# A transformer block on one core: one weight section summed earlier, eight block sums taken out of their product, and the closing row scaling shared out anew

## The chip, the cores and the metric

The kernel runs on one core of one Trainium2 chip. A core has TensorE (PE: matrix products, results in PSUM), VectorE (DVE), ScalarE (ACT), GpSimd (POOL) and SyncE (SP, which here issues most of the DMA transfers). The metric is the device time of one execution in microseconds (us). Three executions of the kernel before took 1255.12, 1257.43 and 1259.67 us, median 1257.43 us.

## The reference

One block of a transformer over 1024 positions of width 1024, in float32: an adaptive normalisation, a mixer with four differential-attention heads and four latent-attention (MLA) heads, a residual with a gate, a second adaptive normalisation, a SwiGLU network, a second gated residual, and a closing normalisation.

```python
mod = c_act @ w_ada[l] + b_ada[l]
sh_a, sc_a, g_a, sh_f, sc_f, g_f = jnp.split(mod[:, None, :], N_MOD, axis=-1)
h = rms_norm(x, g_mix[l]) * (1.0 + sc_a) + sh_a
x = x + g_a * hybrid_mixer(h, w_in[l], ...)
h = rms_norm(x, g_ffn[l]) * (1.0 + sc_f) + sh_f
x = x + g_f * (jax.nn.silu(h @ w_gate) * (h @ w_up)) @ w_down      # D_FF = 2816
return rms_norm(x, g_final)
```

## The kernel before, in words

Each large float32 product is made from three products of rounded halves: an operand is cast by ScalarE to a high part (`dhi`, `whi`), VectorE subtracts to get the low part (`dlo`, `wlo`), both by `split` (L160 to L165, the subtraction is recorded at L158), and TensorE does high by high, high by low and low by high. All tiles that are not small share one pool of 49 slots of 4 KB per partition (`NBUF`, tag "s"); a tile takes a slot when its first instruction is placed and gives it back after its last.

The order of the instructions on an engine is made by a planner. The code emits everything once, and an earlier place in the code is a higher priority; what has its inputs and a slot ready may be placed ahead of what was emitted earlier but is not ready. An instruction passed to `pin` stays behind the instruction that was emitted before it on the same engine. On the chip each engine then works through its list in that order, and waits at an instruction whose input is not there.

Weights come as a `Stream` of items, each a load and a preparation. `pump` emits the next preparation and the loads of the next `ahead` items, `allow` sets how far it may go, `need` goes to a named item at once. The first stream `st` holds what the projections need; `st2` holds w_out and all feed-forward operands.

The stages, in order of time: the input normalisation and the first projections (to 150 us); the latent projections and up-projections as a list `fill`, between which score units of the differential heads are run (150 to 330 us); the other attention units and the first half of the w_out products (to 500 us); w_out and the second normalisation (to 590 us); gate and up products (to 1023 us); down products (to 1243 us); the closing rows.

Section 3 of w_ada (the shift `sh_f`) is 8 loads of 512 KB, each followed by one VectorE multiply-add into `acc` (L339, L341), and after the eighth by 16 small matrix products (L373) and a bias add (L383). It is needed first in the second normalisation. The kernel before keeps it in a stream of its own, `st3`, pumped once in each unit after the first 20, that is while the other attention units run (L1225 to L1227).

The down product uses one level of Strassen's scheme in Winograd's form over the two halves of the 22 rows of blocks: seven products in the order "1256734", each over 11 pairs of blocks c and four row tiles t, three matrix products each (L1484 to L1486). Products alternate between four single PSUM banks (`psb`: 1, 5, 7, 4) and two double ones (`psd`: 2, 6, 3). The operand of product 5 is a sum and a difference of two halves, made by VectorE from two double loads into a tile `stt` (L824 to L827) and then split; products 6, 3 and 4 go on from that tile, and product 7 has two subtractions of its own. `ahead(("dn", i, c), DLEAD)` (L1479) emits preparations up to `DLEAD` items past the one in use and the loads of four items more. Results are taken out of PSUM by closures in `pend`, one after each c (two in product 4): `evac_dn`, `scale` and `base21`. Parts of x1 (the residual) come back from memory by `load_x1`, in product 1 for the row tiles 0 to 3 and in product 7 for the tiles 4 to 7.

In product 4 the last four c are done row tile by row tile, and `last21` (L1455) closes each row: a multiplication by the gate and a subtraction (VectorE, both with an operand in PSUM), a square with its sum (ScalarE), the sum of the two halves' squares (VectorE), two small GpSimd instructions for the reciprocal root, then one half scaled by ScalarE and the other by VectorE, and two DMAs.

Of the kernel before, what the change touches and what calls it, by code (L numbers as in the profile page):

```python
# [10 lines left out]
AF = mybir.ActivationFunctionType  # L11
# [10 lines left out]
LT = 4  # L22
PD = 1
DSP = 2
ALLOW = [(0, 'rope'), (12, ('qup', 2)), (25, None)]
SPILL = 'gpsimd'
DS = 4
ND = 2
# [22 lines left out]
ORD0 = [(1, 1), (0, 1), (0, 2), (1, 2), (0, 2), (0, 0), (0, 0), (0, 0), (1, 0), (1, 0), (1, 0), (1, 0)]  # L51
IT0 = (0, 4, 1, 2, 3, 5, 6, 7)
NLATE = 1
DLEAD = 3


class Stream:
# [40 lines left out]
def emit(ctx, tc, a, out, dbg=None, rec=None):  # L98
# [12 lines left out]
    def slot(shape, dt, name):  # L111
        n = nm(name)
        if rec:
            rec.alloc(n)
        return sp.tile([P] + list(shape), dt, name=n, tag="s", bufs=NBUF)
# [253 lines left out]
    def col_sec(sec, fin):  # L369
        def done(acc):  # L370
            ps = psb()
            for j in range(8):
                pin(mm(ps[:, j:j + 1], lhsT=acc[:, j * 128:(j + 1) * 128], rhs=ones[:, 0:1], start=True, stop=True))  # L373
            fin(ps)

        return ada_items(sec, done)
# [20 lines left out]
    for q in range(3):  # L397
        n = 3 if q < 2 else 2
        witem(st, ("lk", q), win[q * 384:q * 384 + n * 128, 1920:2240].rearrange("(k p) n -> p k n", p=P), [n, 320])
    st.add("rope", load_tabs, lambda: None)  # L400
    for k in range(3):
        witem(st, ("qup", k), a["w_q_up"][k * P:(k + 1) * P, :], [768], nc.gpsimd)
    for k in range(2):
        witem(st, ("kvup", k), a["w_kv_up"][k * P:(k + 1) * P, :], [1024], nc.gpsimd)
    st3 = Stream(2)
    for it in col_sec(3, fin_shf):
        st3.add(*it)


    def x_norm(t):  # L410
# [385 lines left out]
    def dn_item(i, c):  # L796
        key = ("dn", i, c)
        ga = scr["g"][2 * c:2 * c + 2]
        wa = a["w_down"][2 * c * P:(2 * c + 2) * P, :].rearrange("(f p) n -> f p n", p=P)
        g0, g1, w0, w1 = ga[0], ga[1], wa[0], wa[1]  # L800

        def dma():
            r = slot([2, 512], F32, "raw")
            q = None
            if i in "57":
                q = slot([2, 512], F32, "raw")
                if i == "5":
                    ld(out=r, in_=ga[:, :, HI].rearrange("f p t -> p f t"))
                    ld(out=q, in_=w0.rearrange("p (f n) -> p f n", f=2))
                else:  # L810
                    ld(out=r, in_=g0.rearrange("p (f n) -> p f n", f=2))
                    ld(out=q, in_=wa[:, :, HI].rearrange("f p t -> p f t"))
            else:
                x, y = {"1": (g0[:, LO], w0[:, LO]), "2": (g1[:, LO], w1[:, LO]), "6": (g0[:, LO], w1[:, HI]),
                        "3": (g1[:, LO], w1[:, HI]), "4": (g1[:, HI], w1[:, LO])}[i]
                ld(out=r[:, 0, :], in_=x)
                ld(out=r[:, 1, :], in_=y)
            raws[key] = (r, q)

        def prep():  # L820
            r, q = raws.pop(key)
            v = nc.vector
            if i == "5":
                z = stt[c] = slot([2, 512], F32, "stt")  # L824
                v.tensor_tensor(out=z[:, 0, :], in0=r[:, 0, :], in1=r[:, 1, :], op=ALU.add)
                sub(v, z[:, 1, :], q[:, 1, :], q[:, 0, :])
                r = z  # L827
            elif i == "6":
                z = stt[c]
                sub(v, z[:, 0, :], z[:, 0, :], r[:, 0, :])  # L830
                sub(v, z[:, 1, :], r[:, 1, :], z[:, 1, :])
                r = z
            elif i == "7":
                sub(v, r[:, 0, :], r[:, 0, :], r[:, 1, :])
                sub(v, r[:, 1, :], q[:, 1, :], q[:, 0, :])
            elif i == "3":
                sub(v, r[:, 0, :], r[:, 0, :], stt[c][:, 0, :])
            elif i == "4":
                sub(v, r[:, 1, :], stt.pop(c)[:, 1, :], r[:, 1, :])
            hi = slot([2, 512], F32R, "dhi")  # L840
            lo = slot([2, 512], F32R, "dlo")
            split(r, hi, lo)
            W[key] = (hi, lo)

        st2.add(key, dma, prep)
# [62 lines left out]
    ORDER = "1256734"  # L908
    for i in ORDER:
        for c in range(NP):  # L910
            dn_item(i, c)

    def load_t(key, src):
        t = slot([2, 512], F32R, "op")
# [307 lines left out]
    W.clear()  # L1222
    for n in range(done, NS):
        step(n, LA)
        if n > done:  # L1225
            st3.allow()
            st3.pump()  # L1227
        if n - NU in WOL:
            st2.need(("wo", WOL[n - NU]))
        for t in WOD.get(n - NU, []):  # L1230
            wout_d(t)
# [66 lines left out]
    def rest(n, jp):  # L1298
        aop(n, jp, sa[n, jp])
# [154 lines left out]

    def last21(o, t):  # L1455
        t4 = 4 + t
        r = x1[t4]
        vtt(out=o, in0=o, in1=gf[:, LO], op=ALU.mult)
        sub(nc.vector, r[:, LO], r[:, LO], o)
        sq(t4, LO, 0)  # L1460
        ss = ssq[t4]
        vtt(out=ss[:, 0:1], in0=ss[:, 0:1], in1=ss[:, 1:2], op=ALU.add)
        rs = rstd_of(ss[:, 0:1], D)
        nc.scalar.activation(osl[t4][:, HI], r[:, HI], AF.Copy, scale=rs)
        nc.vector.scalar_tensor_tensor(out=osl[t4][:, LO], in0=r[:, LO], scalar=rs, in1=gfin[:, LO], op0=ALU.mult, op1=ALU.mult)
        for half in (HI, LO):
            ld(out=out[t4 * P:(t4 + 1) * P, half], in_=osl[t4][:, half])

    for n, i in enumerate(ORDER):
        if n % 2:  # L1470
            e = [psd() for _ in range(2)]
            o = [e[t // 2][:, t % 2, :] for t in range(4)]
        else:
            o = [psb() for _ in range(4)]
        TL = 7 if i == "4" else NP
        seq = [(c, t) for c in range(TL) for t in range(4)] + [(c, t) for t in range(4) for c in range(TL, NP)]
        for c, t in seq:
            if t == 0:
                ahead(("dn", i, c), DLEAD)  # L1479
                if i in "17" and c in (2, 4, 6, 8):  # L1480
                    load_x1((c - 2) // 2 + (0 if i == "1" else 4))
            hi, lo = W["dn", i, c]
            tt = slice(t * 128, (t + 1) * 128)
            mm(o[t], lhsT=hi[:, 0, tt], rhs=hi[:, 1, :], start=c == 0, stop=False)  # L1484
            mm(o[t], lhsT=hi[:, 0, tt], rhs=lo[:, 1, :], start=False, stop=False)  # L1485
            mm(o[t], lhsT=lo[:, 0, tt], rhs=hi[:, 1, :], start=False, stop=c == NP - 1)  # L1486
            if t == 3:
                del W["dn", i, c]
                for _ in range(2 if i == "4" else 1):
                    if pend:  # L1490
                        pend.pop(0)()
            if i == "4" and c == NP - 1:
                last21(o[t], t)
        if i != "4":
            pend += [lambda i=i, z=z, t=t: evac_dn(i, z, t) for t, z in enumerate(o)]
        if i == "3":
            pend += [lambda t=t: base21(t) for t in range(4)]
    assert not pend


_INS = ["x", "vecs", "ident", "ada_a", "ada_b", "w_ada", "b_ada", "w_in", "rope", "w_q_up", "w_kv_up", "tabs", "lam", "w_out",
# [51 lines left out]
```

## Time and profile before

| | |
|---|---|
| median of three runs | 1257.43 us |
| the profiled execution | 1257.22 us, its span 1255.3 us |
| TensorE busy | 1205.8 us (96%), 5951 products, mean granted clock 0.983 |
| VectorE busy | 829.2 us (66%) |
| ScalarE busy | 494.4 us (39%) |
| GpSimd busy | 439.0 us (35%) |
| chain that ended last | PE 77%, DVE 12%, ACT 4%, no wait shown 4%, DMA 1%, POOL 1% |

All rows are of this one profiled execution, and times in them are microseconds from the start of its span. A busy share over the whole span is a mean over stages with different limits, so the rows below are of single stretches. In a row of instructions the last bracket is the idle time before the first, with what ended it.

### The profile page before, as it was taken

The numbers are of one execution on the slowest core, as the hardware profiler recorded it, in microseconds if no ns is written. First come the engines' busy times: TensorE is split into PE (matmuls) and PEld (weight loads), VectorE is DVE, ScalarE is ACT, GpSimd is POOL, SyncE is SP. The second block draws the span as 40 slices with busy tenths as digits, with TensorE's granted clock in tenths as the row PEclk, the third lists the DMA queues.
The fourth block names the chain that finished last, engine by engine and source line by source line (L and its number), as shares of the span: only waits on it lengthen the run. The fifth ranks groups of instructions, "written<-read, shape, count | busy, mean of one in ns | idle before, by whom it ended". The sixth has DMA issues, their size and how long they took to land.

```text
span 1255.3 us, 16479 instructions
## 1 busy us (share of the span) xinstructions
PE 1205.8 (96%) x5951; PEld 1013.7 (81%) x5951; DVE 829.2 (66%) x1282; ACT 494.4 (39%) x850; POOL 439.0 (35%) x492
## 2 busy tenths in 40 slices
PE   8999999999899999999899999999999999999995
PEld 6888898988679898887688888878888888878774
DVE  6643514477697878768865565665555575699997
ACT  4542225455556665124532223313233244143353
POOL 4420002654243256113455445565444620000112
PEclk9999998999999999999899999999999999999998
DMA  9774842357986434321132233322122369779543
GB/s 369 301 255 167 313 137 74 106 170 227 336 250 166 137 109 144 116 94 59 51 118 96 91 117 125 110 84 84 51 101 84 117 234 393 250 252 327 190 129 135
DMA packets 82972, 209.33 MB, mean 167 GB/s; under 512 B 7805, under 2 KB 18379, under 8 KB 82763
## 3 DMA queue, kind: packets, MB, share of 16 engines
q1 hardware_dynamic: 63611, 168.36, 40.0%
q0 software_dynamic: 6336, 23.07, 4.8%
q10 hardware_dynamic: 12944, 16.84, 3.9%
q8 instruction: 47, 0.77, 0.2%
q14 instruction: 34, 0.28, 0.1%
HBM read 164.21 MB, written 44.04 MB: 166 GB/s over the span
## 4 chain that ended last, share of the span: by engine, by line
PE 77%; DVE 12%; ACT 4%; issue 4%; DMA 1%; POOL 1%; SPq 0%; ACTq 0%; POOLq 0%; DVEq 0%
PE psb L1338 32%; PE psb L439 5%; PE psb L441 5%; PE psb L440 5%; PE psb L481 3%; PE psd L481 3%; PE psd L1485 2%; PE psd L1486 2%; PE psd L1484 2%; PE psb L1030 2%; ACT s L949 2%; PE psb L1485 2%; PE psb L1484 2%; PE psb L1486 2%; DVE dlo L158 1%
## 5 line engine op out<-in xcount | busy, mean ns | idle before, releaser
L1338 PE MATMUL psb<-ah,whi 128*128 128x512 f32 x528 | 143.7, 394 | 2.9 <-ACT uv L1367 2.6
L1338 PE MATMUL psb<-ah,wlo 128*128 128x512 f32 x528 | 142.0, 391 | 0.8 <-DVE wlo L158 0.8
L1338 PE MATMUL psb<-al,whi 128*128 128x512 f32 x528 | 141.7, 390 | 0.4 <-DVE al L158 0.4
L1361 POOL TENSOR_TENSOR cf<-cf,cf 128x512 f32<-128x512 f32 x44 | 66.4, 1510 | 190.5 <-DVE cf L1354 183.9
L1338 PEld LDWEIGHTS psb<-ah,whi 128*128 128x128 f32 x528 | 99.3, 189 | 24.9 <-ACT uv L1367 3.0
L1354 DVE TENSOR_TENSOR cf<-psb,uv 128x512 f32<-128x512 f32 x88 | 60.3, 686 | 89.1 <-PE psb L1338 88.2
L1338 PEld LDWEIGHTS psb<-ah,wlo 128*128 128x128 f32 x528 | 99.6, 189 | 22.1 <-DVE wlo L158 1.2
L1338 PEld LDWEIGHTS psb<-al,whi 128*128 128x128 f32 x528 | 99.0, 188 | 21.4 <-DVE al L158 0.8
L162 ACT CAST whi<-ssum 128x1024 fp32r<-128x1024 f32 x44 | 45.0, 1045 | 166.9 <-POOL ssum L158 166.9
L158 DVE TENSOR_TENSOR wlo<-ssum,whi 128x1024 fp32r<-128x1024 f32 x44 | 62.3, 1416 | 55.5 <-ACT whi L162 55.5
L949 ACT ACTIVATE s<-s,nb 128x640 f32<-128x640 f32 (+7 forms) x96 | 74.4, 777 | 48.9 <-DVE nb L947 48.5
L162 ACT CAST dhi<-raw 128x1024 fp32r<-128x1024 f32 x63 | 64.5, 1051 | 64.5 <-DVE raw L158 29.0
L947 DVE CUSTOM_DVE_ANT_0 s<-psd,tabs 128x640 f32<-128x640 f32 (+7 forms) x80 | 63.3, 803 | 38.2 <-PE psd L973 36.1
L158 DVE TENSOR_TENSOR dlo<-raw,dhi 128x1024 fp32r<-128x1024 f32 x59 | 73.9, 1274 | 15.5 <-ACT dhi L162 15.3
L1485 PE MATMUL psb<-dlo,dhi 128*128 128x512 f32 x176 | 69.0, 392 | 0.1
L439 PE MATMUL psb<-whi,hh 128*128 128x512 f32 (+2 forms) x192 | 68.1, 354 | 1.0 <-ACT latq L638 0.9
L1486 PE MATMUL psb<-dhi,dlo 128*128 128x512 f32 x176 | 68.5, 389 | 0.0
L441 PE MATMUL psb<-whi,hl 128*128 128x512 f32 (+2 forms) x192 | 67.3, 350 | 0.0
L440 PE MATMUL psb<-wlo,hh 128*128 128x512 f32 (+2 forms) x192 | 67.2, 350 | 0.0
L1365 ACT ACTIVATE cf<-cf 128x512 f32<-128x512 f32 x44 | 27.8, 632 | 99.7 <-DVE cf L1354 99.7
L1484 PE MATMUL psb<-dhi 128*128 128x512 f32 x176 | 63.8, 391 | 1.1 <-ACT dhi L162 1.0
L1453 POOL TENSOR_TENSOR x<-x,gfin 128x512 f32<-128x512 f32 x4 | 5.5, 1377 | 164.3 <-ACT o L1417 160.0
(321 smaller groups left out, 3105.9 us busy)
## 6 DMA issues: line engine op xcount, KB each, us to landing
adr<-in_w_ada_dram SPq DMA_DIRECT2D x32, 512.0 KB, 6.4
raw<-scr_g SPq DMA_DIRECT2D x55, 256.0 KB, 3.6
raw<-in_w_down_dram SPq DMA_DIRECT2D x55, 256.0 KB, 4.2
raw<-in_w_gate_dram SPq DMA_DIRECT2D x22, 512.0 KB, 3.3
raw<-in_w_up_dram SPq DMA_DIRECT2D x22, 512.0 KB, 3.3
scr_g<-cf POOLq DMA_DIRECT2D x22, 512.0 KB, 3.2
raw<-scr_g SPq DMA_DIRECT2D x22, 512.0 KB, 5.4
raw<-in_w_down_dram SPq DMA_DIRECT2D x22, 512.0 KB, 6.2
```

Of the source, the lines that this page charges most:

```text
L158: pn(eng.tensor_tensor(out=o, in0=x, in1=y, op=ALU.subtract))
L162: pn(nc.scalar.copy(hi, raw))
L439: mm(o, lhsT=ah, rhs=bh, start=start, stop=False)
L440: mm(o, lhsT=ah, rhs=bl, start=False, stop=False)
L441: mm(o, lhsT=al, rhs=bh, start=False, stop=stop)
L481: pn(mm(o, lhsT=w[z == 2][:, m * 128:(m + 1) * 128], rhs=h[z == 1], start=(k == 0 and z == 0), stop=(k == 7 and z == 2)))
L949: nc.scalar.activation(s, s, AF.Exp, bias=nb[:, m:m + 1], scale=-1.0, accum_out=rs[:, m:m + 1])
L1338: mm(o, lhsT=w[l][:, k, :], rhs=x[2 * (k // 2) + r][:, k % 2, :], start=(l + r == 0 and k == 0), stop=(r == 1 and k == 3))
L1361: nc.gpsimd.tensor_tensor(out=g, in0=g, in1=o, op=ALU.mult)
L1484: mm(o[t], lhsT=hi[:, 0, tt], rhs=hi[:, 1, :], start=c == 0, stop=False)
L1485: mm(o[t], lhsT=hi[:, 0, tt], rhs=lo[:, 1, :], start=False, stop=False)
L1486: mm(o[t], lhsT=lo[:, 0, tt], rhs=hi[:, 1, :], start=False, stop=c == NP - 1)
```

## The change

Three parts. (1) The shift section goes from its own stream into the main one, behind the rope tables and ahead of the up-projection weights; the first `allow` reaches to its end, so its eight items are pumped in the places 4 to 11 of the `fill` list. (2) Product 5's operand is made by separate items "s": for c 0 to 7 they stand at eight places among the items of products 1 and 2 (`EARLY`), for c 8 to 10 just ahead of their use; product 5's item then only splits. The lead in the down product goes from 3 to 6 items, and x1 is loaded in products 2 and 6 instead of 1 and 7. (3) In `last21` the low half is multiplied by the final gain on GpSimd ahead of the scale, the add of the two sums goes to GpSimd, both halves are scaled by ScalarE, and the scaling of a row is emitted after the next row's square; all of it is pinned.

```diff
-ALLOW = [(0, 'rope'), (12, ('qup', 2)), (25, None)]
+ALLOW = [(0, ('ad', 3, 7)), (12, ('qup', 2)), (25, None)]
-DLEAD = 3
+DLEAD = 6
+EARLY = [("1", 3), ("1", 6), ("1", 9), ("2", 1), ("2", 3), ("2", 5), ("2", 7), ("2", 9)]
     st.add("rope", load_tabs, lambda: None)
+    for it in col_sec(3, fin_shf):
+        st.add(*it)
     for k in range(3):
         witem(st, ("qup", k), ...)
...
-    st3 = Stream(2)
-    for it in col_sec(3, fin_shf):
-        st3.add(*it)
...
         def dma():
+            if i == "5":
+                return
             r = slot([2, 512], F32, "raw")
             q = None
-            if i in "57":
+            if i in "s7":
                 q = slot([2, 512], F32, "raw")
...
-            r, q = raws.pop(key)
+            r, q = raws.pop(key, (None, None))
-            if i == "5":
+            if i == "s":
                 z = stt[c] = slot([2, 512], F32, "stt")
                 v.tensor_tensor(out=z[:, 0, :], in0=r[:, 0, :], in1=r[:, 1, :], op=ALU.add)
                 sub(v, z[:, 1, :], q[:, 1, :], q[:, 0, :])
-                r = z
+                return
+            elif i == "5":
+                r = stt[c]
...
     for i in ORDER:
         for c in range(NP):
+            if i == "5" and c >= len(EARLY):
+                dn_item("s", c)
             dn_item(i, c)
+            if (i, c) in EARLY:
+                dn_item("s", EARLY.index((i, c)))
...
         step(n, LA)
-        if n > done:
-            st3.allow()
-            st3.pump()
...
     def last21(o, t):
         t4 = 4 + t
-        r = x1[t4]
-        vtt(out=o, in0=o, in1=gf[:, LO], op=ALU.mult)
-        sub(nc.vector, r[:, LO], r[:, LO], o)
-        sq(t4, LO, 0)
-        ss = ssq[t4]
-        vtt(out=ss[:, 0:1], in0=ss[:, 0:1], in1=ss[:, 1:2], op=ALU.add)
-        rs = rstd_of(ss[:, 0:1], D)
-        nc.scalar.activation(osl[t4][:, HI], r[:, HI], AF.Copy, scale=rs)
-        nc.vector.scalar_tensor_tensor(out=osl[t4][:, LO], in0=r[:, LO], scalar=rs, in1=gfin[:, LO], op0=ALU.mult, op1=ALU.mult)
-        for half in (HI, LO):
-            ld(out=out[t4 * P:(t4 + 1) * P, half], in_=osl[t4][:, half])
+        r, ss, y = x1[t4], ssq[t4], osl[t4]
+        pin(vtt(out=o, in0=o, in1=gf[:, LO], op=ALU.mult))
+        pin(vtt(out=r[:, LO], in0=r[:, LO], in1=o, op=ALU.subtract))
+        pin(nc.scalar.activation(o, r[:, LO], AF.Square, accum_out=ss[:, 0:1]))
+        pin(nc.gpsimd.tensor_tensor(out=y[:, LO], in0=r[:, LO], in1=gfin[:, LO], op=ALU.mult))
+        pin(nc.gpsimd.tensor_tensor(out=ss[:, 0:1], in0=ss[:, 0:1], in1=ss[:, 1:2], op=ALU.add))
+        rs = small(1, "rstd")
+        pin(nc.gpsimd.tensor_scalar(out=rs, in0=ss[:, 0:1], scalar1=1.0 / D, scalar2=EPS, op0=ALU.mult, op1=ALU.add))
+        pin(nc.gpsimd.tensor_tensor(out=rs, in0=rs, in1=mhalf[:, 0:1], op=ALU.pow))
+        for fn in tail:
+            fn()
+
+        def rest():
+            pin(nc.scalar.activation(y[:, HI], r[:, HI], AF.Copy, scale=rs))
+            pin(nc.scalar.activation(y[:, LO], y[:, LO], AF.Copy, scale=rs))
+            for half in (HI, LO):
+                ld(out=out[t4 * P:(t4 + 1) * P, half], in_=y[:, half])
+
+        tail[:] = [rest]
...
-                if i in "17" and c in (2, 4, 6, 8):
-                    load_x1((c - 2) // 2 + (0 if i == "1" else 4))
+                if i in "26" and c in (2, 4, 6, 8):
+                    load_x1((c - 2) // 2 + (0 if i == "2" else 4))
...
-    assert not pend
+    for fn in tail:
+        fn()
```

## Rows read from the trace of the kernel before

**Rows 1.** Windows of the down product: busy us (instructions) by engine, granted clock, DMA share, GB/s.
```profile
1022.90:1082.70 59.80, 59.80 (x265) 49.56 (x264) 33.68 (x33) 18.14 (x20) 3.45 (x4) 1.00 0.95 345
1082.70:1242.90 160.20, 154.68 (x661) 123.84 (x660) 152.08 (x196) 61.84 (x74) 14.54 (x12) 0.99 0.60 206
1173.60:1210.70 37.10, 32.76 (x133) 25.53 (x133) 35.88 (x43) 14.57 (x20) 5.51 (x4) 0.95 0.49 157
1210.70:1242.90 32.20, 31.21 (x133) 24.27 (x131) 30.60 (x41) 12.15 (x18) 9.03 (x8) 1.00 0.28 100
1242.90:1255.30 12.40, 0.04 (x1) 0.00 (x0) 5.62 (x12) 4.84 (x11) 2.95 (x8) 0.66 0.46 170
```
**Rows 2.** Waits of PE in 1170 to 1243 us: us in total, times, longest.
```profile
PE psd L1485 <- DVE dlo L158: 3.4, 3, 1.6
```
**Rows 3.** Timeline of DVE in product 5: start, us, line, tiles.
```profile
1106.96 1.22 DVE L158 TENSOR_TENSOR dlo<-stt,dhi 128x1024 fp32r<-128x1024 f32 x1
1108.10 0.68 DVE L825 TENSOR_TENSOR stt<-raw 128x512 f32<-128x512 f32 x1
1108.70 0.69 DVE L158 TENSOR_TENSOR stt<-raw 128x512 f32<-128x512 f32 x1
```
**Rows 4.** Groups of DVE instructions, first in 1022.9 to 1082.7, then 1082.7 to 1242.9.
```profile
L158 DVE TENSOR_TENSOR dlo<-stt,dhi 128x1024 fp32r<-128x1024 f32 x3 | 3.7, 1225 | 3.5 <-ACT dhi L162 3.5
...
L825 DVE TENSOR_TENSOR stt<-raw 128x512 f32<-128x512 f32 x7 | 4.8, 683 | 0.0
```
**Rows 5.** Window of 1027 to 1077.5 us, and median issue to landing of one load.
```profile
1027.00:1077.50 50.50, 50.50 (x224) 41.85 (x223) 28.70 (x29) 18.14 (x20) 0.00 (x0) 1.00 1.01 372
...
raw<-scr_g SPq DMA_DIRECT2D x55, 256.0 KB, 3.6
```
**Rows 6.** Chain that ended last, 334 to 346 us, then PE's timeline there.
```profile
336.13 7.17 DMA adr<-in_w_ada_dram
...
345.33 0.69 PE L988 MATMUL psb<-E,E 128*128 128x384 f32 x1 [4.00 <-DVE ptl L158]
```
**Rows 7.** Windows in the fill and in the attention units, columns as in Rows 1.
```profile
150.00:175.00 25.00, 25.00 (x125) 22.31 (x124) 2.75 (x4) 3.50 (x8) 0.96 (x4) 1.00 0.64 198
325.00:350.00 25.00, 19.24 (x124) 17.37 (x123) 18.74 (x40) 12.50 (x31) 4.62 (x10) 0.86 1.04 370
345.30:349.20 3.90, 3.87 (x15) 3.78 (x16) 3.90 (x9) 1.10 (x3) 2.94 (x6) 0.50 1.02 405
```
**Rows 8.** Group of the shift section's DVE instructions, 336 to 365 us.
```profile
L341 DVE SCALAR_TENSOR_TENSOR acc<-adr,cact,acc 128x1024 f32<-128x1024 f32 x7 | 8.9, 1278 | 3.5 <-DMA adr<-in_w_ada_dram 3.5
```
**Rows 9.** Page's groups of L162 and L1453, then timelines of POOL and DVE.
```profile
L162 ACT CAST dhi<-raw 128x1024 fp32r<-128x1024 f32 x63 | 64.5, 1051 | 64.5 <-DVE raw L158 29.0 <-DMA raw<-in_w_down_dram 16.7 <-PE psb L1486 6.1
...
L1453 POOL TENSOR_TENSOR x<-x,gfin 128x512 f32<-128x512 f32 x4 | 5.5, 1377 | 164.3 <-ACT o L1417 160.0
...
1180.01 1.28 POOL L1453 TENSOR_TENSOR x<-x,gfin 128x512 f32<-128x512 f32 x1 [153.04 <-ACT o L1417]
...
1180.23 1.62 DVE L158 TENSOR_TENSOR raw<-raw,stt 128x512 f32<-128x512 f32 x1
```
**Rows 10.** Timelines of the closing rows, single engines.
```profile
1240.26 1.30 DVE L1458 TENSOR_TENSOR psb<-psb,gbc 128x512 f32<-128x512 f32 x2 [1.05 <-PE psb L1486]
...
1242.56 0.39 PE L1486 MATMUL psb<-dhi,dlo 128*128 128x512 f32 x1
...
1243.33 0.69 DVE L1458 TENSOR_TENSOR psb<-psb,gbc 128x512 f32<-128x512 f32 x1
...
1246.79 0.68 DVE L158 TENSOR_TENSOR x<-x,psb 128x512 f32<-128x512 f32 x1
...
1249.50 0.19 POOL L221 TENSOR_SCALAR rstd<-ssall 128x1 f32<-128x1 f32 x1 [0.94 <-DVE ssall L1462]
1249.77 0.55 POOL L222 TENSOR_TENSOR rstd<-rstd,mhalf 128x1 f32<-128x1 f32 x1
1250.35 0.72 ACT L1464 ACTIVATE o<-x,rstd 128x512 f32<-128x512 f32 x1 [1.04 <-POOL rstd L222]
```

More of the change, by code (lines that the diff above doesn't have):

```diff
@@ L820, in prep @@
         def prep():
-            r, q = raws.pop(key)
+            r, q = raws.pop(key, (None, None))
             v = nc.vector
-            if i == "5":
+            if i == "s":
                 z = stt[c] = slot([2, 512], F32, "stt")
@@ L1456, in last21 @@
         t4 = 4 + t
-        r = x1[t4]
-        vtt(out=o, in0=o, in1=gf[:, LO], op=ALU.mult)
-        sub(nc.vector, r[:, LO], r[:, LO], o)
-        sq(t4, LO, 0)
-        ss = ssq[t4]
-        vtt(out=ss[:, 0:1], in0=ss[:, 0:1], in1=ss[:, 1:2], op=ALU.add)
-        rs = rstd_of(ss[:, 0:1], D)
-        nc.scalar.activation(osl[t4][:, HI], r[:, HI], AF.Copy, scale=rs)
-        nc.vector.scalar_tensor_tensor(out=osl[t4][:, LO], in0=r[:, LO], scalar=rs, in1=gfin[:, LO], op0=ALU.mult, op1=ALU.mult)
-        for half in (HI, LO):
-            ld(out=out[t4 * P:(t4 + 1) * P, half], in_=osl[t4][:, half])
+        r, ss, y = x1[t4], ssq[t4], osl[t4]
[15 more added lines that the diff above has]
+        tail[:] = [rest]
+    tail = []
     for n, i in enumerate(ORDER):
```

## The prediction

> **What bounds the kernel now.** The page gives TensorE 96% of the span, so a gain can only come from the few stretches where TensorE waits or runs slowly, and from the end after its last product. I read the windows by stage first, to find these stretches, then the chain of waits inside each, then the timelines of the engines that stand in it. Three stretches are touched by the change.
>
> The first is among the attention units. In the window 325 to 350 us TensorE is busy 19.24 of 25 us, and the DMA share is 1.04 [rows 7]. The chain shows why: a load of the shift section takes 7.17 us, VectorE stands at the multiply-add that needs it, and as it works in order the softmax work behind it stands too. TensorE is idle for 4.00 us before L988 [rows 6]. After that gap it runs 3.9 us at a granted clock of 0.50, the lower of its two levels [rows 7].
>
> The second is the down product. The first two of its seven products take 59.8 us with TensorE busy throughout, so one takes 29.9 us when nothing is late. The other five take 160.2 us against 5 x 29.9 = 149.5: 10.7 us are lost, of them 37.1 - 29.9 = 7.2 in product 3 and 32.2 - 29.9 = 2.3 in product 4 [rows 1]. VectorE is the cause: it is busy 152.1 of these 160.2 us, and 35.9 of the 37.1 in product 3 [rows 1], and the longest wait of TensorE there is for a `dlo` [rows 2]. In products 1 and 2 it is busy only 33.7 of 59.8 us [rows 1].
>
> The third is the end. TensorE's last product ends at 1242.56 + 0.39 = 1242.95, the span at 1255.3: 12.35 us in which four rows are closed, and in which VectorE's subtraction of the last row comes at 1246.79, 3.5 us after its multiplication at 1243.33 [rows 10]. Between them VectorE, in order, serves the rows before.
>
> **The change part by part.** The sum is made against the profiled execution, 1257.22 us (span 1255.3), which is 0.2 us from the median 1257.43.
>
> *Shift section.* Removed at the old place: the idle 4.0 us [rows 6], and half of the 3.9 us at half clock, 1.95 [rows 7], together 5.9. VectorE also loses eight multiply-adds, seven of them 8.9 us [rows 8], and the DMA loses 4.2 MB in a stretch where it is full; the other idle time of that window is 25 - 19.24 - 4.0 = 1.8 us [rows 7], and I count 1.6 of it. What is late next there is the softmax chain itself. At the new place the eight multiply-adds lie in a stretch where VectorE is busy 2.75 of 25 us and the DMA share is 0.64 [rows 7]. The latent products that run there are taken out by ScalarE, so VectorE's work has cover until the first scores; then the up-projection loads, the operands of the first score units and the scores follow behind these items, on SP's queue and on VectorE. The 16 small products move along and cost TensorE the same. For delays there I take +1. The bounds: at best nothing is paid at the new place (-7.5), at worst the stall of 5.9 us is met there twice (-7.5 + 11.8 = +4.3). I take -6.5, nearer the first, because VectorE and DMA are both far from full where the items go.
>
> *Early sums and lead.* A sum and a difference start 0.60 us apart, so a pair is 1.2 us; a split is 1108.10 - 1106.96 = 1.14 [rows 3]. Seven pairs lie in the bound stretch [rows 4]; three of them (c 8 to 10) stay near product 5, so 4 x 1.2 = 4.8 us leave it. Before, three splits of product 5 are done when product 2 ends [rows 4]; a lead of six makes it six, 3 x 1.14 = 3.4 us more. VectorE's work in the stretch falls from 152.1 to 143.9 us, below TensorE's 149.5. In products 3 and 4 alone it is 35.9 + 30.6 = 66.5 against 59.8 [rows 1]; three more items ready at their start take off 3 x (0.60 + 1.14) = 5.2 and leave 1.5 too much. With 1.2 for places where work comes in bursts I leave 2.7 of the 10.7 lost: -8. The bounds are -10.7 and, where the planner places the work no differently, 0.
>
> What hides the moved work: VectorE has 59.8 - 33.7 = 26 us free in products 1 and 2 [rows 1]. The DMA has less: it is full from 1027 to 1077.5 us (1.01, 372 GB/s [rows 5]). Products 1 and 2 need 22 items of 0.524 MB, the eight early sums 8 x 1.05 and x1 2.1 MB, 22.0 MB in all, and 372 GB/s over 59.8 us give 22.2. It fits only just, with what is loaded before 1022.9 as the reserve, so I count nothing; each MB too much would cost 2.7 us. The loads of x1 move by one product and stay one product (29.9 us) ahead of their use, nothing.
>
> *Closing rows.* From TensorE's end: 0.38 to VectorE's start, 0.60 and 0.69 for its two instructions [rows 10]; then GpSimd's multiplication, 1.38 [rows 9], which outlasts ScalarE's square beside it; then the add (0.19, by the nearest row, L221), 0.19 and 0.55 with three gaps of 0.08 [rows 10]: 1.17; then ScalarE twice 0.72; then from its end to the span's end what it is now, 1255.3 - 1251.07 = 4.2 [rows 10], less 0.4, an estimate, as the first half's DMA is out already. Sum 9.5 against 12.35: -2.9. But GpSimd now spends 1.38 + 1.17 = 2.55 us on each row, and the rows end 12 x 0.226 = 2.7 us apart on TensorE at best. Where rows come together, as now (the first multiplication at 1240.26 [rows 10]), four rows take 10.2 us on GpSimd: 1240.26 + 1.3 + 10.2 + 1.44 + 3.8 = 1257.0, that is +1.7. I take -2, nearer the good end as the second part should leave VectorE little late.
>
> GpSimd's four multiplications can also slow VectorE. The row: beside L1453 a subtraction of two SBUF tiles took 1.62 us instead of 0.69 [rows 3, 9]. The Trainium skill says so too (GPSIMD Engine Reference, section 8, Key points): GpSimd shares its SBUF interfaces with VectorE and contends with VectorE instructions that have two SBUF inputs. By that rule, with which the trace agrees, each new multiplication would cost 0.93 us if such an instruction lay beside it, 3.7 us in four rows, and the sum would be 1244.4, inside the forecast's own range. VectorE's two instructions in a closing row have one operand in PSUM, so I count nothing.
>
> Sum: 1257.2 - 6.5 - 8 - 2 = 1240.7, so **1241 us**.
>
> **The rivals.** *VectorE stays the bound.* Instructions are placed by a planner that sees priorities, not by the code's order, and pinned rows stand behind everything emitted before them. If the lead does not grow, only the four pairs are gained, 4.8 us less the bursts, say 3, and the rows still come together: 0 for the end. 1257.2 - 6.5 - 3 = 1248. For it: VectorE is 95% busy in the stretch and stays at 96% of TensorE's time. Against it: the work removed is more than its idle time lacks.
>
> *The wait moves along.* The shift items wait at their new place as they did at the old one: 1257.2 - 8 - 2 = 1247. For it: TensorE has no slack there (25.00 of 25 [rows 7]) and an idle stretch lowers its clock too. Against it: DMA share 0.64 against 1.04.
>
> *Slots run out, slower.* The place is products 6, 7 and 3. In product 3 tiles that stay hold 29 of 49 slots (two gains, four sums, eight x1, eleven `stt`, four `o`), and seven prepared pairs hold 14: six are left for loads. An item takes 3.6 us to load [rows 5], 1.05 for its cast [rows 9], 0.60 and 1.2 on VectorE [rows 3], 6.5 us in all, against 2.72 us (29.9/11) in which TensorE uses one. It decides where fewer than 6.5 / 2.72 = 2.4 items are under way: at 1.8, an item takes 3.6 us, 0.9 late, over 33 items 30 us: 1241 + 30 = 1271. For it: tiles are held longer (x1, `stt`, deeper lead). Against it: six are left where 2.4 do.
>
> *Nothing that can be measured.* The first two rivals together: 1257.2 - 3 = 1254 to 1261.
>
> **How the numbers follow.** Forecast 0.56 (its own range 1235 to 1247), VectorE still the bound 0.18, the wait moves along 0.13, nothing 0.06, slots 0.07. A difference of 0.3%, 3.8 us, is about what a measurement of this kernel tells from none. Faster by more (below 1253.7): 0.56 + 0.18 + 0.13 = 0.87; same 0.06; slower 0.07. The range that holds 8 in 10: 0.13 lies above 1253, and with the upper edge of the first rival about 0.16 above 1252; some 0.03 lies below 1231, where all three parts reach their best ends (1257.2 - 7.5 - 10.7 - 2.9 = 1236) and the attention units gain more than their idle time. So 1231 to 1252.
>
> **What would show it.** Right: no gap before L988 and no clock of 0.50 near 342 us; `acc` in 155 to 205 us without new idle time of TensorE; products 5, 6, 7 at 30 us and 3 and 4 together at 62.5 instead of 69.3; 9.5 to 11 us from the last product to the end, with GpSimd's multiplication in the chain that ended last. Wrong: `dlo` still ahead of TensorE's gaps in product 3; a wait for `raw` loads in products 1 or 2; an idle TensorE between 185 and 205 us; the four closing rows on GpSimd back to back.

## The result, and the profile after

The changed kernel takes 1244.18 us (median of 4 runs, 1242.92 to 1245.65) against 1256.28 us (4 runs, 1254.55 to 1259.67): ratio 0.990, 95% interval 0.987 to 0.993. That is 12 us faster; 1241 was forecast, 16 us less than the 1257.43 us that three executions of the kernel before had given. The profiled execution took 1245.65 us, its span is 1243.4, 11.9 less than the span of before.

To see where, the span is cut at three instructions that every kernel here has: the first latent product (here the start of the fill, at about 120 us), the first matrix product of the down stage, and the end of the last one. The figures are differences of these times in the traces, in us. "Units" holds the fill, the attention units, w_out, gate and up. The kernels e1 to e12 are the experiments below; there is one trace of each.

| kernel | start | units | down | end | down + end |
|---|---|---|---|---|---|
| before | 120.1 | 902.8 | 220.0 | 12.4 | 232.4 |
| after | 122.6 | 895.9 | 209.6 | 15.3 | 224.9 |
| e1 shift section alone | 121.8 | 894.7 | 218.8 | 12.1 | 230.8 |
| e2 sums, lead and x1 alone | 122.7 | 899.1 | 209.6 | 14.4 | 224.0 |
| e3 closing rows alone | 122.1 | 898.9 | 220.1 | 13.0 | 233.2 |
| e4 after, old closing rows | 123.7 | 896.0 | 209.6 | 14.7 | 224.3 |
| e5 after, lead 3 | 120.6 | 895.7 | 216.2 | 13.0 | 229.2 |
| e6 after, lead 8 | 120.0 | 896.4 | 209.6 | 14.4 | 224.0 |
| e7 after, rows shared | 121.9 | 895.5 | 209.6 | 14.1 | 223.7 |
| e8 after, scalings late | 124.1 | 895.9 | 209.6 | 15.7 | 225.3 |
| e9 lead 8, rows shared | 119.9 | 895.9 | 209.6 | 13.4 | 223.0 |
| e10 lead 8, rows on VectorE | 124.4 | 895.9 | 209.6 | 14.0 | 223.6 |
| e11 as e10, two scalings off VectorE | 123.6 | 896.3 | 213.4 | 11.9 | 225.4 |
| e12 after, no GpSimd product behind 7 | 120.0 | 895.9 | 209.6 | 13.5 | 223.1 |

Against the profiled run of before, the changed kernel has +2.5 at the start, -6.9 in the units, -10.4 in the down stage and +2.9 at the end. The start is no part of the change: the kernels with one and the same code up to there (after, e1, e4 to e12) start the fill between 119.9 and 124.4 us. Windows of the changed kernel, for [rows 1] and [rows 7]; columns as there:

```profile
150.00:175.00 25.00, 25.00 (x122) 21.88 (x121) 10.56 (x12) 3.66 (x7) 1.87 (x2) 1.00 0.76 245
...
325.00:350.00 25.00, 23.54 (x157) 21.04 (x156) 20.82 (x50) 17.01 (x40) 4.61 (x13) 1.00 0.97 335
341.00:346.00 5.00, 4.75 (x40) 4.62 (x40) 3.79 (x10) 2.81 (x7) 1.80 (x6) 1.00 0.80 251
...
1018.50:1078.40 59.90, 59.90 (x266) 49.61 (x265) 39.90 (x42) 24.11 (x26) 3.47 (x4) 1.00 0.91 329
1078.40:1228.10 149.70, 149.70 (x661) 123.70 (x659) 142.06 (x182) 57.78 (x67) 16.41 (x12) 1.00 0.62 210
1168.10:1198.00 29.90, 29.90 (x133) 24.78 (x132) 29.90 (x37) 12.46 (x18) 5.65 (x4) 1.00 0.56 178
1198.00:1228.10 30.10, 30.10 (x133) 24.60 (x132) 30.10 (x40) 11.87 (x16) 10.76 (x8) 1.00 0.22 81
...
1228.10:1243.40 15.30, 0.02 (x1) 0.00 (x0) 4.92 (x8) 8.01 (x16) 8.53 (x16) 0.64 0.51 192
```

TensorE is busy 23.54 us in 325 to 350 where it was busy 19.24, at full clock around 342 us. In the down stage it never waits: 149.70 of 149.70 us in the last five products, and the wait of [rows 2] is gone. But VectorE is busy 29.90 of 29.90 and 30.10 of 30.10 us in the last two. It is exactly full there, and what it can't finish waits for the end (e12 tests this). VectorE's timeline there, for [rows 10] (start, us, line, tiles):

```profile
1224.17 3.66 DVE L1447 SCALAR_TENSOR_TENSOR o<-x,rstd,gfin 128x1024 f32<-128x1024 f32 x3
1227.76 0.68 DVE L1463 TENSOR_TENSOR psb<-psb,gbc 128x512 f32<-128x512 f32 x1
1228.48 0.69 DVE L1464 TENSOR_TENSOR x<-x,psb 128x512 f32<-128x512 f32 x1
1229.08 0.69 DVE L1463 TENSOR_TENSOR psb<-psb,gbc 128x512 f32<-128x512 f32 x1
```

Row 0's first multiplication (1227.76) comes right behind three scalings (L1447), with no idle time between, 0.4 us before TensorE's last product ends at 1228.12; the rows then follow 1.33 us apart. GpSimd's timeline, the first row and the last, then ScalarE's last scaling:

```profile
1229.31 1.27 POOL L1466 TENSOR_TENSOR o<-x,gfin 128x512 f32<-128x512 f32 x1 [4.65 <-DVE x L1464]
1230.53 0.19 POOL L1467 TENSOR_TENSOR ssall<-ssall 128x1 f32<-128x1 f32 x1
1230.81 0.19 POOL L1469 TENSOR_SCALAR rstd<-ssall 128x1 f32<-128x1 f32 x1
1231.09 0.55 POOL L1470 TENSOR_TENSOR rstd<-rstd,mhalf 128x1 f32<-128x1 f32 x1
1231.60 1.27 POOL L1466 TENSOR_TENSOR o<-x,gfin 128x512 f32<-128x512 f32 x1
...
1236.19 1.27 POOL L1466 TENSOR_TENSOR o<-x,gfin 128x512 f32<-128x512 f32 x1
...
1239.18 0.70 ACT L1476 ACTIVATE o<-o,rstd 128x512 f32<-128x512 f32 x1
```

GpSimd takes 1231.60 - 1229.31 = 2.29 us for each row, with no pause, while VectorE brings one every 1.33 us: 9.2 us for four rows, the larger part of the 15.3.

One wait is new. TensorE's waits in 185 to 205 us, then two pieces of the chain that ended last:

```profile
PE psd L980 <- DVE nb L955: 3.0, 3, 2.1
```
```profile
194.61 1.19 DVE acc L342
195.80 0.47 DVE s L955
```

A score product waits 2.1 us for the softmax before it, and that stands behind a multiply-add of the shift section, which is now here. Two older waits, for `latq`, are shorter in return (0.3 and 0.6 us, where they were 1.6 and 0.9): TensorE's idle time between 150 and 210 us rises from 2.5 to 3.9 us.

### The profile page after: what moved, and what is told of

Read it like the earlier page. It is cut to its first block, busy times and chain, and to the rows that moved or that the text cites. A ratio compares the mean times of both kernels' runs of the same rounds, so it can differ in the third digit from the quotient of the medians.

```text
span 1243.4 us, 16505 instructions
## 1 busy us (share of the span) xinstructions
PE 1201.7 (97%) x5951; PEld 1014.9 (82%) x5951; DVE 824.8 (66%) x1274; ACT 498.1 (40%) x854; POOL 443.5 (36%) x500
## 4 chain that ended last, share of the span: by engine, by line
PE 79%; DVE 11%; ACT 3%; issue 3%; DMA 2%; POOL 1%; SPq 0%; ACTq 0%; POOLq 0%; DVEq 0%
PE psb L1343 32%; PE psb L439 5%; PE psb L441 5%; PE psb L440 5%; PE psb L481 3%; PE psd L481 3%; PE psb L1498 2%; PE psb L1500 2%; PE psb L1499 2%; PE psb L1038 2%; PE psd L1498 2%; PE psd L1500 2%; PE psd L1499 2%; ACT s L957 1%; DVE dlo L159 1%
## 5 line engine op out<-in xcount | busy, mean ns | idle before, releaser
L1343 PE MATMUL psb<-ah,whi 128*128 128x512 f32 x528 | 143.9, 394 | 2.8 <-ACT uv L1372 2.6
L1343 PE MATMUL psb<-ah,wlo 128*128 128x512 f32 x528 | 142.1, 391 | 0.8 <-DVE wlo L159 0.8
L1499 PE MATMUL psb<-dlo,dhi 128*128 128x512 f32 x176 | 68.5, 389 | 0.0
L1500 PE MATMUL psb<-dhi,dlo 128*128 128x512 f32 x176 | 68.5, 389 | 0.0
L1498 PE MATMUL psb<-dhi 128*128 128x512 f32 x176 | 66.7, 389 | 0.0
```

Of the source, the lines that this page charges most:

```text
L1343: mm(o, lhsT=w[l][:, k, :], rhs=x[2 * (k // 2) + r][:, k % 2, :], start=(l + r == 0 and k == 0), stop=(r == 1 and k == 3))
```

## The experiments

Theory: the three parts add up; the third costs time, because GpSimd sets the end, and the second hands part of its gain to the end, because VectorE is full. The rivals stand in each expectation. Kernels before ran beside each: 1255.31 us for e1 to e8, 1254.97 for e9 to e12. Most of the 95% intervals below are 8 to 10 us wide (4 to 7 us for e1, e2, e3, e5 and e8), wider than many of the differences between these kernels. Differences of 2 us and less are read from the traces, one execution each.

**e1, the shift section alone.**

```
-    st3 = Stream(2)
-    for it in col_sec(3, fin_shf):
-        st3.add(*it)
+    for it in col_sec(3, fin_shf):      # before w_q_up
+        st.add(*it)
...
-            st3.allow()
-            st3.pump()
```

> The kernel before with the shift section moved and nothing else of the change. Theory (parts add up): TensorE's gap before the scores and the stretch at the lower clock go (8.5 us), the fill pays some 1.6 us, the down product keeps its 160 us for the last five products and its end its 12.4 us: 7 us less than before, about 1249 us. Rival 1 (the 2.5 us that the changed kernel's profiled run lost in its first 34 us belong to the moved section): 4.5 us less, about 1252. Rival 2 (the wait moves along and stays): no more than 3 us less, 1253 or more.

1250.0 us, ratio 0.996 (0.994 to 0.998): 5.3 us less. The gap is gone, as in the changed kernel:

```profile
325.00:350.00 25.00, 23.54 (x157) 21.04 (x156) 20.89 (x50) 17.00 (x40) 4.34 (x13) 1.00 0.96 333
```

The time fits rival 1 better than the theory, but not its reason: e2 and e3 leave the section where it was and start as late (122.7 and 122.1). The reason is that the profiled run of before was slow in two places of the units. The same wait at the same place was 4.0 us there [rows 6], and 2.0 and 3.1 us in the traces of e2 and e3:

```profile
344.41 0.44 PE L997 MATMUL psb<-E,E 128*128 128x384 f32 x1 [2.03 <-DVE ptl L159]
```
```profile
343.62 0.68 PE L988 MATMUL psb<-E,E 128*128 128x384 f32 x1 [3.09 <-DVE ptl L158]
```

The other place is 175 to 215 us. The three kernels do the same there and TensorE has the same two waits for `latq`, 1.6 and 0.9 us, but its mean granted clock was 0.91, 0.96 and 1.00 (before, e2, e3), that is, it was at the lower of its two levels for a part of the stretch in before and e2 and not in e3:

```profile
175.00:215.00 40.00, 37.48 (x213) 36.13 (x212) 13.52 (x47) 16.58 (x52) 6.62 (x21) 0.91 0.27 73
175.00:215.00 40.00, 37.48 (x220) 36.13 (x219) 13.54 (x47) 16.23 (x51) 6.37 (x20) 0.96 0.35 91
175.00:215.00 40.00, 37.33 (x228) 35.74 (x226) 14.00 (x49) 17.64 (x55) 7.61 (x25) 1.00 0.32 88
```

Counted from the start of the fill and without the wait itself, the product behind the wait comes after 221.2, 219.7 and 218.4 us. So of the 3.7 us that e2's units are shorter than those of before, 1.5 lie ahead of the wait and 2.0 in it; of e3's 3.9, 2.8 and 0.9. Why the clock differed is not shown. The three traces with the section at its old place need 902.8, 899.1 and 898.9 us for the units, mean 900.3; the eleven with the new place 894.7 to 896.4, mean 895.8. The section's move is worth 4.4 us by these means; single traces at the old place differ by 3.9.

**e2, sums, lead and x1 alone; e3, closing rows alone; e4, the changed kernel with the old rows.**

```
-DLEAD = 3
+DLEAD = 6
+EARLY = [("1", 3), ("1", 6), ("1", 9), ("2", 1), ...]        # e2: and dn_item, load_x1
-        vtt(out=o, in0=o, in1=gf[:, LO], op=ALU.mult)
+        pin(vtt(out=o, in0=o, in1=gf[:, LO], op=ALU.mult))   # e3: the whole new last21
```

> The kernel before with the early sums, the lead of six and the later loads of x1, but the shift section at its old place and the old closing rows. Theory (parts add up): all seven products at 29.9 us, the gap among the attention units unchanged, the end no longer than 12.4 us: 10.4 us less than before, about 1246 us. Rival 1 (the products gained because the shift section's move let the pairs be loaded earlier): at least one of the last five products stays over 31 us, gain 5 us or less, 1251. Rival 2 (VectorE is full in the last product, so what it is behind shows in the end instead): products flat, but 15 us or more from the last product to the end, gain 7.5 us, 1249.

> The kernel before with the new closing rows and nothing else of the change. Theory (GpSimd is the bound of the new rows, some 2.3 us for each of four, and they start when VectorE comes to them, as late as now): from the first multiplication at 1240.3 us 1.5 + 4 x 2.3 + 1.4 + 4.2 us to the end, some 1 to 2 us more than before, about 1257.5 us, with the four rows back to back on GpSimd. Rival (the prediction): the rows stand 2.7 us apart and GpSimd keeps up, 2 us less, about 1254.

> The changed kernel with the closing rows of the kernel before. Theory (the new rows cost time): the seven products stay at 29.9 us, and from the last product to the end it takes 11 to 12.4 us instead of 15.3: about 3 us less than the changed kernel, 1241 us. Rival (VectorE is full in the last product with either ending, and the old rows give it more to do behind it): 15 us or more at the end, the same as the changed kernel or slower, 1244 to 1247 us.

e2: 1246.24 us, ratio 0.993 (0.990 to 0.995). All seven products at 29.9 us, so they owe nothing to the first part; rival 1 falls. At the end 14.4 us where 12.4 were: rival 2 is right in kind, though 2.0 us more is less than it had. The median is the theory's 1246, but the theory had no longer end. VectorE's timeline in e2 shows the same three scalings ahead of row 0, with the old rows too:

```profile
1227.47 3.66 DVE L1451 SCALAR_TENSOR_TENSOR o<-x,rstd,gfin 128x1024 f32<-128x1024 f32 x3
1231.06 1.28 DVE L1467 TENSOR_TENSOR psb<-psb,gbc 128x512 f32<-128x512 f32 x2
```

e3: 1255.42 us, ratio 1.000 (0.998 to 1.002); the end is 13.0 us, 0.7 more, and the rival's 2 us less are not seen. On GpSimd, as in the changed kernel, the rows are back to back, 1246.85 - 1239.94 = 3 x 2.30 us:

```profile
1239.94 1.29 POOL L1461 TENSOR_TENSOR o<-x,gfin 128x512 f32<-128x512 f32 x1 [12.81 <-DVE x L1459]
...
1246.85 1.27 POOL L1461 TENSOR_TENSOR o<-x,gfin 128x512 f32<-128x512 f32 x1
```

e4: 1244.42 us, ratio 0.990 (0.986 to 0.994), the same as the changed kernel, and 14.7 us at the end. The rival is right: VectorE's lateness, not the new rows, makes most of the longer end. The new rows cost 0.7 us in the old surroundings (e3 against before) and 0.6 in the new ones (after against e4), by single traces.

**e5 and e6, the lead.** In the changed kernel `DLEAD = 3`, then `DLEAD = 8`.

> The changed kernel with the lead put back from six items to three; the eight early sums stay. Theory (both halves of the second part are needed): without the lead VectorE has three prepared items fewer when products 3 and 4 begin, 3 x (0.60 + 1.14) = 5.2 us, so product 3 takes about 33 to 35 us again, the last five products together 154 to 156 us instead of 149.6: 5 us slower than the changed kernel, about 1249. Rival (moving the pairs is enough, since 4 x 1.2 us leave a stretch that was 2.6 us too full): all products at 29.9 us, within 1 us of the changed kernel.

> The changed kernel with a lead of eight items instead of six. Theory (VectorE's 6.7 us of idle time before product 6's first sum is there because no further item may be prepared): two more items are prepared in it, 2 x (0.60 + 1.14) = 3.5 us of VectorE's work leave the last product, the rows begin earlier and the end takes 12 to 13.5 us instead of 15.3: about 2.5 us faster, 1241.5. Rival (slots run out: two more pairs hold four more slots): loads come late, gaps of TensorE with a wait for a cast or a load in products 5 to 7, slower than 1246.

e5: 1248.1 us, ratio 0.995 (0.994 to 0.997). Windows of the last three products, and TensorE's longest wait in the stage:

```profile
1135.90:1166.80 30.90, 30.75 (x134) 24.60 (x134) 30.80 (x41) 12.65 (x12) 0.00 (x0) 1.00 0.80 272
1166.80:1199.40 32.60, 30.55 (x134) 24.51 (x133) 32.60 (x41) 13.72 (x19) 5.66 (x4) 1.00 0.50 160
1199.40:1232.50 33.10, 31.40 (x133) 24.18 (x131) 31.42 (x42) 12.18 (x17) 11.95 (x9) 1.00 0.29 102
```
```profile
PE psd L1499 <- DVE dlo L159: 2.0, 2, 1.6
```

The wait for `dlo` is back, and the down stage takes 6.6 us more than in the changed kernel. The theory holds: of the 10.4 us, 220.0 - 216.2 = 3.8 come with the eight pairs and 6.6 with the lead. The later loads of x1 went with the pairs in every run, and have no price of their own. But the end is 2.3 us shorter: where TensorE waits, VectorE is less behind when it stops. It even waits for TensorE's row 0, until 2.7 us before the last product's end (1232.45):

```profile
1229.77 0.70 DVE L1463 TENSOR_TENSOR psb<-psb,gbc 128x512 f32<-128x512 f32 x1 [1.06 <-PE psb L1500]
```

Of the 6.6 us 4.3 are left (medians: 3.9).

e6: 1242.69 us, ratio 0.991 (0.987 to 0.995), not to be told from the changed kernel by its times. The end is 0.9 us shorter, not 2.5:

```profile
1221.28 3.66 DVE L1447 SCALAR_TENSOR_TENSOR o<-x,rstd,gfin 128x1024 f32<-128x1024 f32 x3
1224.87 0.68 DVE L1463 TENSOR_TENSOR psb<-psb,gbc 128x512 f32<-128x512 f32 x1
```

Row 0 still stands behind the scalings, at 1.1 us before the last product's end instead of 0.4. The premise was wrong: VectorE's idle time in product 6 went only from 6.7 to 5.8 us. It is a sum at the head of its queue that waits for the product's result, and prepared items don't pass it. From product 5 on neither TensorE nor VectorE waits for a load with the lead of eight, so slots don't run out.

**e7 to e9, the end.** e7 keeps GpSimd's multiplication for row 0 alone:

```
-        pin(nc.gpsimd.tensor_tensor(out=y[:, LO], in0=r[:, LO], in1=gfin[:, LO], op=ALU.mult))
+        if t in (0,):
+            pin(nc.gpsimd.tensor_tensor(...))      # rows 1 to 3, after row 3's drain:
+            pin(nc.vector.scalar_tensor_tensor(out=y[:, LO], in0=r[:, LO], scalar=rs, in1=gfin[:, LO], ...))
```

e8 has `late.append(scale)` for `pend.append(scale)`, and runs `late` after the last rows; e9 is e7 with `DLEAD = 8`.

> The changed kernel with GpSimd's multiplication kept for row 0 of the last four alone; the second halves of rows 1 to 3 are scaled by VectorE in one instruction each, after the fourth row is drained. Theory (GpSimd sets the end: 4 x 2.29 us in a row from 1229.3): three multiplications of 1.27 us leave it, the last power is done near 1235, VectorE's last scaling near 1235.7, about 3.7 us less at the end: 1240.5. Rival (VectorE's lateness and the transfers set the end): less than 1 us less, 1243.5 or more.

> The changed kernel with the four scalings of rows 0 to 3 (four times 1.2 us on VectorE) put behind the last four rows instead of in front of them. Theory (row 0's first multiplication stands behind these scalings on VectorE, which is full in the last product): it starts at 1226 instead of 1227.8, all four rows move up by it, and the scalings fill VectorE's idle time behind: 1.7 us less at the end, 1242.5. Rival (it is TensorE's order that sets when the rows end, so nothing moves up): within 0.5 us, or later where the scalings' own transfers now end last.

> The changed kernel with the lead of eight and with GpSimd's multiplication kept for row 0 of the last four alone (the two earlier edits together). Theory (they act on different parts of the end: when the rows begin, and how long GpSimd takes for them): from the last product to the end 13.2 us, where the lead alone left 14.4 and the shared rows alone 14.2: 1242. Rival (both move the same wait): 14 us or more, no faster than the lead alone.

e7: 1243.11 us, ratio 0.991 (0.988 to 0.995); the end is 1.2 us shorter, nearer the rival's number than the theory's 3.7. Here and below the first half of a row is the columns 512 to 1023 (`HI`), which are sent first, and the second half the columns 0 to 511 (`LO`). VectorE's last scaling, then the transfers on SP's queue behind it:

```profile
1235.52 0.75 DVE L1485 SCALAR_TENSOR_TENSOR o<-x,rstd,gfin 128x512 f32<-128x512 f32 x1 [1.00 <-POOL rstd L1471]
...
1236.69 0.88 SPq L1486 DMA_DIRECT2D out_dram<-o  x2
```

The last scaling ends 1236.27, 9.2 us after the last product; ScalarE's last one in the changed kernel ended 11.8 us after it (1239.88 - 1228.12). Of these 2.5 us 1.4 are lost on the way out: the second half of row 2, scaled by 1234.5, is issued only at 1236.69, behind row 3's first half, and row 3's second half behind it.

e8: 1244.8 us, ratio 0.992 (0.989 to 0.994), and an end of 15.7 us: the rival's later end, but not for its reason. The scalings are not pinned, and the planner set two of them between the drains:

```profile
1227.62 0.70 DVE L1464 TENSOR_TENSOR psb<-psb,gbc 128x512 f32<-128x512 f32 x1 [0.66 <-PE psb L1501]
1228.22 1.28 DVE L1448 SCALAR_TENSOR_TENSOR o<-x,rstd,gfin 128x1024 f32<-128x1024 f32 x1
1229.42 0.68 DVE L1465 TENSOR_TENSOR x<-x,psb 128x512 f32<-128x512 f32 x1
```

Row 0 starts 2.0 us before TensorE's end, 1.6 earlier than in the changed kernel, as the theory wants and as soon as TensorE has it, and is then cut in two. Whether pinned late scalings would gain was not tried.

e9: 1241.14 us (1240.36 to 1242.14), ratio 0.988 (0.985 to 0.992), end 13.4 us where 13.2 was expected: the two edits add up. It has the fastest median of all kernels here, 3.0 us below the changed kernel's; the intervals overlap, and the traces account for 1.9 us.

**e10 to e12, contention** (instructions that are longer beside another engine's). e10 has the lead of eight, drops GpSimd's multiplication in all four rows and pins the order: four drains and squares, then all scalings (first halves on ScalarE, second halves on VectorE) and transfers. e11 is e10 with

```
+                if t in (2, 3):
+                    nc.gpsimd.tensor_tensor(out=osl[t], in0=x1[t], in1=gfin, op=ALU.mult)
+                    nc.scalar.activation(osl[t], osl[t], AF.Copy, scale=rs)
```

and e12 is the changed kernel without `base21`'s last line, `nc.gpsimd.tensor_tensor(out=rh, in0=rh, in1=gfin[:, HI], ...)`: it leaves the final gains out of the first halves of the last four rows.

> The changed kernel with the lead of eight, no multiplication of GpSimd in the last four rows: first all four rows are drained, squared and their powers taken, then ScalarE scales the first halves and VectorE the second ones, and the transfers are issued in that order. Theory (GpSimd's multiplications, and squares that wait on ScalarE behind the scaling of earlier rows, set the end): VectorE drains until 4.2 us after the last product as with the lead alone, the last power comes 1.8 us later, the last scaling near 7.5 us, the last transfer is issued near 7.9 us and lands 2.8 us later: 11.8 us at the end, 3.5 us less than the changed kernel, 1240.7. Rival (the order of issue or the landing of eight transfers at once sets the end): 13 us or more.

> As the run before it in this call, and two of the four scalings of rows 0 to 3 are taken from VectorE: GpSimd multiplies by the gains and ScalarE by the row's factor. Theory (VectorE is the engine that is late when the last product ends): it comes to row 0 up to 2.4 us earlier, as far as the rows are ready by then, so some 0.6 to 1.5 us less at the end. Rival (GpSimd's two multiplications of 128x1024 lengthen VectorE's subtractions of two SBUF tiles beside them, as the four smaller ones do, by 0.4 to 1 us for each): nothing gained or up to 2 us lost, with subtractions of 1.6 us and more in the last 12 us of the last product.

> The changed kernel without GpSimd's four multiplications of 128x512 behind product 7 (the first halves of the last four rows leave out the final gains). Theory (these four lengthen the VectorE instructions with two SBUF inputs that lie beside them, 1.64 for 1.22 and 1.62 for 0.68 us, 2.9 us in all): none of VectorE's instructions in products 3 and 4 is longer than its kind elsewhere, and VectorE reaches the last four rows up to 2.9 us earlier, of which 1 to 1.5 us shows at the end, as the rows are not ready before: 1243. Rival (the long ones are long for another reason): they stay, and so does the time.

e10: 1243.42 us, ratio 0.990 (0.986 to 0.994), end 14.0, against 14.4 with the lead of eight alone (e6). GpSimd's third power, VectorE's last scaling, SP's queue:

```profile
1234.26 1.01 POOL L1469 TENSOR_TENSOR rstd<-rstd,mhalf 128x1 f32<-128x1 f32 x1
...
1236.91 0.75 DVE L1473 SCALAR_TENSOR_TENSOR o<-x,rstd,gfin 128x512 f32<-128x512 f32 x1 [0.71 <-POOL rstd L1469]
...
1235.60 4.47 SPq L1475 DMA_DIRECT2D out_dram<-o  x8
```

The last scaling ends 7.8 us after the last product (at 1229.90), as the theory had it (7.5). But eight transfers now wait together, and issuing them takes 4.47 us: the last is issued at 1239.5, 9.6 instead of 7.9 us after the last product. The rival is right. In the changed kernel they were issued as the rows came, so the queue was never the bound.

e11: 1244.07 us, ratio 0.991 (0.988 to 0.995); down and end together 1.7 us more than e10, in the traces; the medians (0.65 us apart) can't tell the two. GpSimd and VectorE, and TensorE's wait:

```profile
1218.54 2.40 POOL L1448 TENSOR_TENSOR o<-x,gfin 128x1024 f32<-128x1024 f32 x1
...
1218.94 3.17 DVE L1459 TENSOR_TENSOR uw<-uw,gbc 128x512 f32<-128x512 f32 x2
1222.02 3.50 DVE L1460 TENSOR_TENSOR x<-uw,x 128x512 f32<-128x512 f32 x2
```
```profile
PE psb L1500 <- DVE dlo L159: 1.9, 1, 1.9
```

Two pairs that take 1.28 us each elsewhere took 3.17 and 3.50 beside GpSimd's multiplications: 4.1 us lost to save 2.4. The rival is right.

e12: 1242.08 us, ratio 0.989 (0.986 to 0.992), end 13.5, 1.8 less than the changed kernel. VectorE reaches row 0 early and waits for TensorE:

```profile
1218.76 3.67 DVE L1447 SCALAR_TENSOR_TENSOR o<-x,rstd,gfin 128x1024 f32<-128x1024 f32 x3
1223.43 0.70 DVE L1461 TENSOR_TENSOR psb<-psb,gbc 128x512 f32<-128x512 f32 x1 [1.01 <-PE psb L1498]
```

The theory holds. In the changed kernel the pair looks like this, as in [rows 9], and below it is the same kind of subtraction in e12:

```profile
1180.91 1.29 POOL L1458 TENSOR_TENSOR x<-x,gfin 128x512 f32<-128x512 f32 x1 [2.58 <-ACT o L1422]
...
1181.13 1.62 DVE L159 TENSOR_TENSOR raw<-raw,stt 128x512 f32<-128x512 f32 x1
```
```profile
1182.24 0.68 DVE L159 TENSOR_TENSOR raw<-raw,stt 128x512 f32<-128x512 f32 x1
```

No VectorE instruction in e12's last two products is longer than its kind elsewhere. But VectorE had to wait for row 0 until 2.0 us before the last product's end (1225.43), and the rows still came 1.33 us apart.

## Why the prediction was right in sign and 3 us too fast

By stages that the experiments price, the change is -4.4 (section) - 7.7 (sums and lead: down and end together fall by 8.4 from before to e2, by 6.5 from e1 to e4 and by 8.3 from e3 to after, on the mean 7.7) + 0.7 (rows) = -11.4, beside -12.1 measured. The forecast had -6.5 - 8 - 2 = -16.5. So 4 to 5 us of the gain are missing, more than the 3 us by which 1241 is off: the median of before, from which it was counted, is 1.2 us lower with its fourth execution. The prices are from single traces; that of the sums and lead came out between 6.5 and 8.4.

*Shift section: right in mechanism, the sum mis-sized.* At the old place the stall went as described. Its size was read from one execution, and that one had the longest of the three waits now known; the units of that execution are 6.9 us longer than the changed kernel's, near the -6.5, but those of e2 and e3 only 3.2 and 3.0. At the new place +1 was taken for delays, and TensorE's idle time there grew by 1.4 us, with one wait of 2.1 behind a multiply-add. Not all eight fall into 150 to 175 us, where VectorE has room: five do (L340 and L342, 169.4 to 175.5), and three come at 192 to 203 us, among the first scores.

*Early sums and lead: right in sum, wrong in form.* The price, -8, was right, and so was counting both halves (e5). But I left 2.7 us of TensorE waiting in products 3 and 4; nothing waits there, and the excess of VectorE's work appears at the end instead (+2.0 in e2). VectorE's work in the five products is 142.1 us where 143.9 was worked out; in the last two it still fills every microsecond.

*Closing rows: the step that failed.* "I take -2, nearer the good end as the second part should leave VectorE little late." It came out at the bad end, +0.7. From the last product to the end it took 15.3 us, not 9.5 to 11, and the sign of being wrong, four rows back to back on GpSimd, is there. The good end needs rows that leave TensorE 2.7 us apart, and the prediction took VectorE's lateness for the reason that they come together. But TensorE brings them together: rows 2.7 us apart would have had row 0 ready some 8 us before the last product ends, and VectorE waited for it until 2.7 us before that end in the kernel before [rows 10] and in e5, until 2.0 in e12. The code emits the last products row by row, but in the trace they are mixed; in the changed kernel three first products (L1498) follow each other, where a single row tile would take all three kinds (L1498, L1499, L1500) in turn:

```profile
1223.65 0.84 PE L1498 MATMUL psb<-dhi 128*128 128x512 f32 x3
```

So the rows come to VectorE almost together and leave it 1.33 us apart, late (in the changed kernel) or not (e3, e12), and GpSimd's 2.29 us a row is the bound either way. Relieving VectorE, which the second part was to do, did not bring the good end (e12: 13.5 us). The bound of +1.7 had the right mechanism, with 2.55 us a row. Less work on GpSimd alone gains little, though: 1.2 us in e7, where the transfers then wait for each other.

*The rivals.* VectorE stays the bound: it does, but its excess is moved to the end, not into the products. The wait moves along: partly, 2.1 us. Slots run out: no, not even with a lead of eight. GpSimd's new multiplications beside VectorE: counted at nothing for the drains, which have one operand in PSUM; they take 0.68 and 0.69 us beside L1466, as without (e10). The Trainium skill has a rule for this (SBUF — State Buffer, Who interferes with whom): a VectorE instruction with at most one SBUF input, outside what the page calls 2-port perf modes, does not contend with GpSimd, and one with two SBUF inputs contends with a GpSimd instruction that reads SBUF. The traces agree with both halves: those two drains, and the pairs in e11 and the subtraction that is short again in e12. That the prediction's 1244.4, with four drains slowed, lies beside the measured 1244.18 is chance: none is slowed.

## What to carry to other kernels

An engine that is exactly full in the last stage can leave no stall there and hand its arrears to the end, as VectorE does here: after relieving it, read down stage and end together. Work moved to a slower engine at the end is priced by that engine's time per row against the distance of the rows as they arrive in the trace, not as the code writes them. The length of a wait for a transfer needs more than one execution before it is booked as a gain: here one wait was 4.0, 3.1 and 2.0 us in three traces. The times spread wider where it stands, too: 11.5 us in e2 (8 runs) and 8.1 in e3 (10 runs), against 4.7 in e1 and 3.9 in e5 (10 runs each), which have the section at the new place.

## What the hardware showed that was not expected

- Contention went both ways: beside VectorE's scalings of two SBUF tiles GpSimd's power on 128x1 took 1.01 us instead of 0.55 (e10), and beside GpSimd's multiplications VectorE's pairs took 3.17 and 3.50 us instead of 1.28 (e11).
- With the same instructions in the same order and the same waits of TensorE, its mean granted clock between 175 and 215 us was 0.91, 0.96 and 1.00 in the traces of before, e2 and e3, and e2 and e3 came 1.5 and 2.8 us earlier to the wait at 340 us (e1).
- Transfers issued alone, as in the changed kernel, take SP's queue 0.33 us each; eight in a row took 4.47 us, 0.56 each (e10).
- The time to the fill differs by 4.5 us between executions (119.9 to 124.4) among kernels with the same code up to there.
